# Moving the low parts of the key, query and rotated-head evacuations into the weight stream of a two-layer hybrid decoder kernel

## The chip, the cores and the metric

One core of a Trainium2 chip runs the whole kernel. The metric is the device time of one execution in microseconds (us); 1863.25 us is the median of three runs before the change (1862.83 to 1863.87).

## The reference, cut to what matters

Two layers over a sequence of 1024 tokens with 1024 channels. Each layer norms the stream, projects it by one wide matrix, feeds four mixers (stick-breaking attention, a grouped state-space model called S5, retention, and a gated linear recurrence called RG-LRU), gates and projects each mixer's output, sums them and projects once more.

```python
h = _rms_norm(x, pre_g)
proj = jnp.einsum('bsd,dc->bsc', h, w_in)
sb_qkv, ssm_u, ret_qkv, lru_u, gates, merge = jnp.split(proj, SPLITS, axis=-1)
...
# stick-breaking attention, per block of 128 queries
q = q.astype(jnp.float32) * (d ** -0.5)
z = jnp.einsum('bhqd,bhkd->bhqk', q[:, :, lo:hi], k[:, :, :hi])
...
# retention: q and k are rotated first
return jnp.concatenate([t1 * cos - t2 * sin, t1 * sin + t2 * cos], axis=-1)
```

## The kernel before, in words

The work is cut into four units, one for each layer and half sequence of 512 tokens: unit 0 (layer 0, first half), unit 1 (layer 0, second half), unit 2 and unit 3 (layer 1). A unit is a fixed series of 64 weight tiles, i = 0 to 63, of 1024 or 1280 columns each, handled by `filler` (L1133). Every product is made three times in a reduced-precision float (`mm3`, L1110): high part of the activations by high part of the weights, low by high, high by low. So each half tile of weights is loaded by SyncE, and then split by `split` (L106): ScalarE copies it to the high part `wh` (L86), VectorE subtracts that from the raw weights and writes the low part `wl` (L89). There are five buffers for each part. `ahead(g, hf)` (L207) keeps this stream three half tiles ahead of TensorE: at half tile s it issues the split of half tile s+3. In a half tile of 12 matmuls the third is the first that reads `wl`.

This text numbers half tiles within a unit: tile i has the halves 2i and 2i+1. So the split of half 27 (second half of tile 13) is issued at the start of tile 12, that of half 28 in the middle of tile 12.

All engines work in the order in which the code emits their instructions. Around a tile this is: the steps of the side generators that a hand-written plan (`PLAN`, L1475) puts at the start of the tile; the split of the first half and 12 matmuls; the split of the second half, `mid` (L1453, more side steps) and 12 matmuls; then the evacuation of the finished PSUM bank. The tiles that matter here are:

- i = 8 and 10 (L1165): keys of stick-breaking attention. ScalarE copies two high halves into `kS` (L1172), VectorE subtracts two low halves (L1176).
- i = 9 and 11 (L1179): queries. ScalarE makes eight scaled copies of 64 x 128 (L1195), VectorE makes eight scaled duplicates (`ts`, L1197) and eight low parts (`stt`, L1199). Eight more ScalarE copies of the low parts (`rest`, L1201) are kept in `S["late"]` and emitted in the `mid` of the next tile.
- i = 12 to 15 (L1225): queries and keys of retention, rotated. ScalarE makes four shifted copies (L1237), VectorE multiplies by the cosine (L1238), multiplies the shifted copy by the sine (L1239) and adds (L1240).

The stick-breaking attention `sba` (L989) is started at i = 12. At the start of tile 12 TensorE makes the scores of the first block and head, and ScalarE two sigmoids of each segment (L1040, L1041), with a table load in front. In the middle of tile 12 VectorE makes the scans and products on them (L1053 to L1059). At the start of tile 14 TensorE transposes the result (L1019). The second head follows from tile 14 on in the same way. The RG-LRU steps (`lru`, L706) and S5 steps (`s5`, L768) lie between them; in unit 0 also the preparation of the S5 tables (`prep`, L468) with transposes at L630.

The queries, keys and rotated heads use PSUM banks from `A` (three buffers), tile 8 one from `B` (five buffers).

Of the kernel before, what the change touches and what calls it, by code (L numbers as in the profile page):

```python
# [9 lines left out]
F32 = mybir.dt.float32  # L10
# [4 lines left out]
ALU = mybir.AluOpType  # L15
# [28 lines left out]
def hybrid_kernel(ctx: ExitStack, tc: tile.TileContext, x, xt, ws1, ws2, par, bcw, preg, postg, con, rot, out, dbg=None):  # L44
# [17 lines left out]
    def nm(s):  # L62
        cnt[0] += 1
        return f"{s}{cnt[0]}"

    def G(dt=F32, w=512):
        return genp.tile([P, w], dt, tag="g", name=nm("g"))

    def A():
        return psa.tile([P, 512], F32, tag="a", name=nm("pa"))  # L70
# [8 lines left out]
    def Bdone(n=1):  # L79
        bopen[0] -= n  # L80

    def actv(out, in_, func, **kw):
        act.activation(out, in_, func, **kw)  # L83

    def copy(out, in_, **kw):
        act.activation(out, in_, AF.Copy, **kw)  # L86

    def tt(out, a, b, op):
        dve.tensor_tensor(out, a, b, op=op)  # L89

    def ts(out, a, s1, s2=None, op0=ALU.mult, op1=None):
        if s2 is None:
            dve.tensor_scalar(out, a, s1, None, op0=op0)  # L93
        else:
            dve.tensor_scalar(out, a, s1, s2, op0=op0, op1=op1)

    def stt(out, a, s, b, op0, op1):
        dve.scalar_tensor_tensor(out, in0=a, scalar=s, in1=b, op0=op0, op1=op1)  # L98

    def mm(out, lhsT, rhs, start=True, stop=True):  # L100
        pe.matmul(out, lhsT=lhsT, rhs=rhs, start=start, stop=stop)  # L101
# [4 lines left out]
    def split(src, hi, lo):  # L106
        copy(hi, src)
        tt(lo, src, hi.bitcast(F32), ALU.subtract)
# [19 lines left out]
    kS = [const.tile([P, SEQ], F32R, name=f"kS{h}") for h in range(4)]  # L128
# [28 lines left out]
    def tile_of(u, i):  # L157

        if i < GATE0:
            return 0, i  # L160
        if i >= WOUT0:
            return 0, i - 4 * 8
        n, j = group(u, i), (i - GATE0) % GRP
        return (1, 8 * n + j - 2) if j >= 2 else (0, GATE0 + 2 * n + j)
# [6 lines left out]
    def load_to(g):  # L171
        while nload[0] <= min(g, ntot - 1):
            u, i = divmod(nload[0], NTILE)
            kind, idx = tile_of(u, i)
            src = (ws1, ws2)[kind]
            w = 2 * HALF[kind]
            t = rawp.tile([P, w], F32, tag="raw", name=nm("raw"))
            if nload[0]:
                sp.dma_start(t, src[units[u][0], idx])
            else:  # L180
                for hf in range(2):
                    sp.dma_start(t[:, hf * w // 2:(hf + 1) * w // 2], src[units[u][0], idx][:, hf * w // 2:(hf + 1) * w // 2])
            raws[nload[0]] = t
            nload[0] += 1

    def split_to(s):
        while nsplit[0] <= min(s, 2 * ntot - 1):
            g, hf = divmod(nsplit[0], 2)
            load_to(g)
            kind = tile_of(*divmod(g, NTILE))[0]  # L190
            w = HALF[kind]
            hi = whp.tile([P, w], F32R, tag="wh", name=nm("wh"))
            lo = wlp.tile([P, w], F32R, tag="wl", name=nm("wl"))
            split(raws[g][:, hf * w:(hf + 1) * w], hi[:, :], lo[:, :])
            his[nsplit[0]] = hi
            los[nsplit[0]] = lo
            if hf:
                raws.pop(g)
            nsplit[0] += 1
# [7 lines left out]
    def ahead(g, hf):  # L207
        load_to(g + 3)
        split_to(2 * g + hf + 3)

    def wdone(g):
        for s in (2 * g, 2 * g + 1):
            his.pop(s)
            los.pop(s)


    S = {}


    def prologue(u):  # L220
# [64 lines left out]
    def set_h(hh, hl):  # L285
        S["h"] = ([hh[:, k, :] for k in range(KD)], [hl[:, k, :] for k in range(KD)])

# [23 lines left out]
    def prologue_t(c):  # L311
        gc = S["par", 0][:, C_PG:C_PG + 8]
        xk = [G() for _ in range(KD)]
# [30 lines left out]
    def first():  # L344
        pr = S["par", 0] = parp.tile([P, NPAR], F32, tag="par", name=nm("par"))
        gc = pr[:, C_PG:C_PG + 8]
# [17 lines left out]
        for k in range(KD):  # L364
# [8 lines left out]
            if k < 4:  # L373
                sqs.append(G())
                actv(sqs[k], xk[k], AF.Square)
        S["h"] = (xh, xl)
        yield 0
# [17 lines left out]
        for k in range(0, KD, 2):  # L395
# [6 lines left out]
            if k == 2:  # L402
                set_h(hh, hl)
                for t in range(2):
                    dve.memset(uext[t][:, 0:3], 0.0)
                    tt(uext[t][:, 3:3 + T], S.pop(("lps", t)), rb, ALU.mult)
                    S["uext", t] = True
                    Bdone()
# [714 lines left out]
    def coltile(g, mid, side=False):  # L1123
        ps = B() if side else A()
        for hf in range(2):
            ahead(g, hf)
            if hf:
                mid()
            for k in range(4 * hf, 4 * hf + 4):
                mm3(ps, g, k * P, P, False, hsl(k), k == 0, k == 7)  # L1130
        return ps

    def filler(u, i, mid):  # L1133
        l, c = units[u]
        g = u * NTILE + i
# [14 lines left out]
        elif i < 4:  # L1150
            t = i - 2
            ps = coltile(g, mid, i == 2 or u == 0)
# [12 lines left out]
        elif i in (8, 10):  # L1165
            pq = i // 10
            ps = coltile(g, mid, i == 8)
            for h2 in range(2):
                k_ = kS[2 * pq + h2]
                a = slice(64 * h2, 64 * h2 + 64)  # L1170
                cs = slice(ts0, ts0 + T)
                copy(k_[a, cs], ps[a, :])  # L1172
            for h2 in range(2):
                k_ = kS[2 * pq + h2]
                a, b = slice(64 * h2, 64 * h2 + 64), slice(64 - 64 * h2, 128 - 64 * h2)
                tt(k_[b, cs], ps[a, :], k_[a, cs].bitcast(F32), ALU.subtract)  # L1176
            if i == 8:
                Bdone()
        elif i in (9, 11):  # L1179
            pq = i // 11  # L1180
            ps = coltile(g, mid)
            todo = []
            for b in range(NT):
# [4 lines left out]
                for h2 in range(2):  # L1188
                    a = slice(64 * h2, 64 * h2 + 64)
                    h = 2 * pq + h2  # L1190
                    hs_ = slice(h * P, (h + 1) * P)
                    o = slice(64 - 64 * h2, 128 - 64 * h2)
                    todo.append((qh[a, hs_], qh[o, hs_], ql[a, hs_], ql[o, hs_], ps[a, sl]))
            for q_, _, _, _, z in todo:
                copy(q_, z, scale=0.125)  # L1195
            for _, qd, _, _, z in todo:
                ts(qd, z, 0.125)  # L1197
            for q_, _, r_, _, z in todo:
                stt(r_, z, 0.125, q_.bitcast(F32), ALU.mult, ALU.subtract)  # L1199

            def rest():  # L1201
                for _, _, r_, rd, _ in todo:
                    copy(rd, r_.bitcast(F32))

            S["late"] = rest
        elif i < 8:
            if i == 4:
                S["vps"] = [A(), A(), A(), B()]
# [7 lines left out]
            if i == 7:  # L1216
                ps = S.pop("vps")
# [7 lines left out]
        elif i < GATE0:  # L1225
            j = i - 12
            pq, isk = divmod(j, 2)
# [4 lines left out]
            ps = coltile(g, mid)  # L1232
            cs, sn = S["rot"]
            sw, r = G(), G()
            for b in range(4):
                a = b ^ 1
                copy(sw[32 * b:32 * b + 32, :], ps[32 * a:32 * a + 32, :])  # L1237
            tt(r, ps, cs, ALU.mult)  # L1238
            tt(sw, sw, sn, ALU.mult)  # L1239
            tt(r, r, sw, ALU.add)  # L1240
            S[("rk" if isk else "rq"), pq] = r
            if j == 3:
                S.pop("rot")
# [1 line left out]
        elif i < WOUT0:  # L1245
            n, j = group(u, i), (i - GATE0) % GRP
            if j < 2:
                ps = coltile(g, mid)
# [8 lines left out]
            else:  # L1257
                d = j - 2
# [22 lines left out]
        else:  # L1281
# [32 lines left out]
            else:  # L1314
                ps = S["ops"]
                o, st = S["o"]
# [81 lines left out]
    todo = {}  # L1398
# [27 lines left out]
    with tc.manual_schedule():  # L1426
        dve.memset(ones1, 1.0)
        warm = G(BF16)
        dve.memset(warm, 0.0)
        ps = A()  # L1430
        for _ in range(NWARM):
            mm(ps, warm[:, 0:P], warm)
        start("first", first())
        for t in (tmat, ore, oim, wll):
            pool.memset(t if t is not wll else t.bitcast(F32), 0.0)
        for u, (l, c) in enumerate(units):
            for i in range(NTILE):
                if u == 0 and i == 8:
                    copy(identb, ident)
                    copy(trib, cons[:, K_TRI:K_TRI + P])  # L1440
                if i == 12:
                    start("sb", sba(l, c))
                if i == 28 and c == 1 and l + 1 < DEPTH:
                    load_par(l + 1)
                for name, f in (("post", WOUT0), ("prep", NTILE if u else 24), ("lru", GATE0), ("s5", GATE0 + (1 if u else 2) * GRP),
                                ("ret", GATE0 + (2 if u else 1) * GRP), ("sb", GATE0 + 3 * GRP)):
                    if i == f:
                        drain(name)

                sb_now = i % 2 == 0  # L1450
                hfree[0] = i > WOUT0

                def mid():  # L1453
                    finish_gate()
                    if "late" in S:
                        S.pop("late")()
                    step("first")
                    if sb_now:
                        step("sb")
                    planned(u, 2 * i + 1)  # L1460

                if sb_now:
                    step("sb")
                planned(u, 2 * i)
                filler(u, i, mid)
                step("first")
            drain("prep")
            drain("pro")
# [157 lines left out]
```

## Time and profile before

| | |
|---|---|
| median of three runs | 1863.25 us |
| the profiled execution's own time | 1862.88 us |
| its span, first to last instruction | 1861.1 us |
| TensorE (PE) busy | 1826.2 us, 98% |
| VectorE (DVE) busy | 1200.8 us, 65% |
| ScalarE (ACT) busy | 888.2 us, 48% |
| GpSimd (POOL) busy | 258.1 us, 14% |
| mean granted TensorE clock | 0.995 |

A busy share is an average over stages: an engine that is busy 65% of the span can be the bound for 30 us on end. A row of a timeline gives the start, the duration, the engine, the line, what is written from what, and in brackets how long the engine had stood idle before and which engine's instruction ended that. A row that ends in x8 stands for eight instructions in a row.

### The profile page before, as it was taken

What the parts mean: (1) busy time and instruction counts of PE and PEld (TensorE: products, weight loads), DVE (VectorE), ACT (ScalarE), POOL (GpSimd) and SP (SyncE); (2) the same over time, 40 slices, a digit from 0 to 9 for tenths busy, and PEclk for the clock granted to TensorE, in tenths of its full rate; (3) what the DMA queues carried; (4) which work ended last, traced back from release to release, by engine and by line L of the source; (5) the groups of instructions that cost most, each with busy time, mean ns of one, the idle gap of its engine ahead of it and who ended that gap; (6) DMA issues with size and microseconds to landing.
All of it is one profiled execution on the core that took longest, in us unless ns stands there. A gap on an engine that the chain in (4) does not pass through costs nothing.

```text
span 1861.1 us, 24840 instructions
## 1 busy us (share of the span) xinstructions
PE 1826.2 (98%) x9210; PEld 1508.6 (81%) x9210; DVE 1200.8 (65%) x2168; ACT 888.2 (48%) x1673; POOL 258.1 (14%) x573
## 2 busy tenths in 40 slices
PE   9989999999999999999999999999999999999997
PEld 6767888888888888888888788888888788888886
DVE  7777755455689576744558856656437895676445
ACT  5773444344476444544546543344353845444333
POOL 6891000020000002893000000000000000000001
PEclk9999999999999999999999999999999999999999
DMA  5231232324333222232434322242243323222232
GB/s 177 99 119 48 71 125 87 125 94 154 104 132 103 89 81 71 87 135 91 145 112 136 100 90 95 78 138 99 94 139 123 118 85 102 69 78 71 99 105 102
DMA packets 68856, 193.95 MB, mean 104 GB/s; under 512 B 9600, under 2 KB 18176, under 8 KB 68736
## 3 DMA queue, kind: packets, MB, share of 16 engines
q1 hardware_dynamic: 68736, 192.38, 30.9%
q8 instruction: 72, 1.18, 0.3%
q14 instruction: 48, 0.39, 0.1%
HBM read 179.11 MB, written 12.58 MB: 103 GB/s over the span
## 4 chain that ended last, share of the span: by engine, by line
PE 85%; DVE 8%; ACT 5%; issue 1%; DMA 1%; SPq 0%; DVEq 0%; ACTq 0%
PE pa L101 66%; PE pb L101 16%; DVE g L89 2%; PE pb L1019 2%; ACT g L86 2%; ACT g L83 1%; DVE wl L89 1%; DVE g L98 1%; DVE g L93 1%; ACT wh L86 1%; DMA raw<-in_ws_dram 1%; DVE g L810 0%; PE pb L254 0%; ACT kS L86 0%; DVE g L1057 0%
## 5 line engine op out<-in xcount | busy, mean ns | idle before, releaser
L101 PE MATMUL pa<-hh,wl 128*128 128x512 f32 x1576 | 616.2, 391 | 13.3 <-DVE wl L89 13.3
L101 PE MATMUL pa<-hh,wh 128*128 128x512 f32 x1576 | 624.1, 396 | 0.1
L101 PE MATMUL pa<-hl,wh 128*128 128x512 f32 x1576 | 615.0, 390 | 0.0
L89 DVE TENSOR_TENSOR wl<-raw,wh 128x512 fp32r<-128x512 f32 (+1 forms) x512 | 374.7, 770 | 196.0 <-ACT wh L86 195.2
L89 DVE TENSOR_TENSOR g<-g,g 128x512 f32<-128x512 f32 (+7 forms) x435 | 298.8, 687 | 124.3 <-ACT g L86 104.6
L86 ACT ACTIVATE wh<-raw 128x512 fp32r<-128x512 f32 (+1 forms) x512 | 328.3, 686 | 85.6 <-PE pb L101 42.5
L101 PEld LDWEIGHTS pa<-hh,wl 128*128 128x128 f32 x1576 | 296.6, 188 | 80.0 <-DVE wl L89 16.7
L101 PEld LDWEIGHTS pa<-hh,wh 128*128 128x128 f32 x1576 | 296.7, 188 | 61.3 <-ACT wh L86 0.5
L101 PEld LDWEIGHTS pa<-hl,wh 128*128 128x128 f32 x1576 | 296.9, 188 | 58.3 <-DVE hl L89 0.2
L83 ACT ACTIVATE g<-pa 128x512 f32<-128x512 f32 x161 | 96.3, 598 | 507.1 <-PE pa L101 464.6
L89 DVE TENSOR_TENSOR g<-g,pa 128x512 f32<-128x512 f32 x128 | 87.6, 685 | 189.6 <-PE pa L101 171.2
L101 PE MATMUL pa<-g,wh 128*128 128x512 f32 x544 | 169.2, 391 | 2.4 <-ACT g L83 1.1
L905 POOL MEMSET g<- 128x512 f32 x8 | 4.0, 526 | 938.2 <-PE pb L101 937.1
L86 ACT ACTIVATE g<-pb 128x512 f32<-128x512 f32 (+4 forms) x163 | 72.8, 472 | 123.6 <-PE pb L101 88.4
L101 PEld LDWEIGHTS pa<-g,wh 128*128 128x128 f32 x544 | 102.0, 188 | 26.6 <-ACT g L83 1.9
L86 ACT ACTIVATE g<-g 128x512 fp32r<-128x512 f32 (+2 forms) x152 | 79.3, 522 | 72.6 <-DVE g L89 34.9
L101 PE MATMUL pa<-g,wl 128*128 128x512 f32 x272 | 106.0, 390 | 0.0
L83 ACT ACTIVATE g<-pb 128x512 f32<-128x512 f32 (+4 forms) x203 | 87.9, 513 | 22.4 <-PE pb L101 19.6
L86 ACT ACTIVATE g<-pa 64x128 fp32r<-64x128 f32 (+3 forms) x150 | 69.1, 461 | 34.5 <-PE pa L101 32.9
L101 PE MATMUL pa<-wh,g 128*128 128x512 f32 x256 | 79.5, 392 | 0.0
L101 PE MATMUL pb<-wh,g 128*128 128x512 f32 x256 | 79.1, 391 | 0.0
L83 ACT ACTIVATE g<-g 128x512 f32<-128x512 f32 (+2 forms) x98 | 57.1, 602 | 31.1 <-DVE g L89 22.8
(215 smaller groups left out, 2093.8 us busy)
## 6 DMA issues: line engine op xcount, KB each, us to landing
raw<-in_ws_dram SPq DMA_DIRECT2D x128, 640.0 KB, 3.9
raw<-in_ws_dram SPq DMA_DIRECT2D x127, 512.0 KB, 3.7
g<-x SPq DMA_DIRECT2D x32, 256.0 KB, 5.9
g<-in_xt_dram SPq DMA_DIRECT2D x16, 256.0 KB, 6.7
g<-in_x_dram SPq DMA_DIRECT2D x16, 256.0 KB, 3.1
x<-g SPq DMA_DIRECT2D x16, 256.0 KB, 2.1
out_dram<-g SPq DMA_DIRECT2D x16, 256.0 KB, 2.0
g<-in_rot_dram SPq DMA_DIRECT2D x8, 256.0 KB, 4.3
```

What stands on the lines that cost most here:

```text
L83: act.activation(out, in_, func, **kw)
L86: act.activation(out, in_, AF.Copy, **kw)
L89: dve.tensor_tensor(out, a, b, op=op)
L93: dve.tensor_scalar(out, a, s1, None, op0=op0)
L98: dve.scalar_tensor_tensor(out, in0=a, scalar=s, in1=b, op0=op0, op1=op1)
L101: pe.matmul(out, lhsT=lhsT, rhs=rhs, start=start, stop=stop)
L905: pool.memset(t, 0.0)
L1019: pe.transpose(ps[:, q * P:(q + 1) * P], r[:, q * P:(q + 1) * P], ident)
```

## The change

The low parts are no longer emitted at once after the high copies. They are put into a list, and `ahead` takes one entry from it at each half tile, right after the split of that half tile. A query tile gives three entries: low parts and duplicates of the first two blocks; those of the last two blocks and the four ScalarE copies for the first two; the four ScalarE copies for the last two. A key tile gives one entry (both subtractions), a rotated tile one (sine product and sum). The copies no longer wait for `mid`. No instruction is added or removed.

```diff
     def ahead(g, hf):
         load_to(g + 3)
         split_to(2 * g + hf + 3)
+        if S["later"]:
+            S["later"].pop(0)()
...
-            for h2 in range(2):
-                k_ = kS[2 * pq + h2]
-                a, b = slice(64 * h2, 64 * h2 + 64), slice(64 - 64 * h2, 128 - 64 * h2)
-                tt(k_[b, cs], ps[a, :], k_[a, cs].bitcast(F32), ALU.subtract)
-            if i == 8:
-                Bdone()
+
+            def lows():
+                for h2 in range(2):
+                    k_ = kS[2 * pq + h2]
+                    a, b = slice(64 * h2, 64 * h2 + 64), slice(64 - 64 * h2, 128 - 64 * h2)
+                    tt(k_[b, cs], ps[a, :], k_[a, cs].bitcast(F32), ALU.subtract)
+                if i == 8:
+                    Bdone()
+
+            S["later"].append(lows)
...
             for q_, _, _, _, z in todo:
                 copy(q_, z, scale=0.125)
-            for _, qd, _, _, z in todo:
-                ts(qd, z, 0.125)
-            for q_, _, r_, _, z in todo:
-                stt(r_, z, 0.125, q_.bitcast(F32), ALU.mult, ALU.subtract)
-
-            def rest():
-                for _, _, r_, rd, _ in todo:
-                    copy(rd, r_.bitcast(F32))
-
-            S["late"] = rest
+
+            def share(o, d):
+
+                def run():
+                    for q_, _, r_, _, z in o:
+                        stt(r_, z, 0.125, q_.bitcast(F32), ALU.mult, ALU.subtract)
+                    for _, qd, _, _, z in o:
+                        ts(qd, z, 0.125)
+                    for _, _, r_, rd, _ in d:
+                        copy(rd, r_.bitcast(F32))
+                return run
+
+            S["later"] += [share(todo[:4], []), share(todo[4:], todo[:4]), share([], todo[4:])]
...
             tt(r, ps, cs, ALU.mult)
-            tt(sw, sw, sn, ALU.mult)
-            tt(r, r, sw, ALU.add)
+
+            def turn():
+                tt(sw, sw, sn, ALU.mult)
+                tt(r, r, sw, ALU.add)
+
+            S["later"].append(turn)
...
                 def mid():
                     finish_gate()
-                    if "late" in S:
-                        S.pop("late")()
                     step("first")
```

## Rows read from the trace of the kernel before

**Rows 1.** The page: busy time of each engine, share of the span, instructions.
```profile
PE 1826.2 (98%) x9210; PEld 1508.6 (81%) x9210; DVE 1200.8 (65%) x2168; ACT 888.2 (48%) x1673; POOL 258.1 (14%) x573
```

**Rows 2.** Whom TensorE waited for: us in total, times, longest us.
```profile
PE pa L101 <- DVE wl L89: 13.5, 8, 4.2
```

**Rows 3.** Timeline of TensorE in unit 1, tiles 13 and 14.
```profile
555.99 0.50 PE L101 MATMUL pa<-hh,wl 128*128 128x512 f32 x1 [0.87 <-DVE wl L89]
...
558.16 0.39 PE L101 MATMUL pa<-hh,wl 128*128 128x512 f32 x1
559.44 0.76 PE L1019 MATMUL pb<-cons,g 128*128 128x128 f32 x5 [0.89 <-DVE g L89]
```

**Rows 4.** Timeline of ScalarE in unit 1, tiles 9 to 12.
```profile
538.07 2.57 ACT L86 ACTIVATE g<-g 64x128 fp32r<-64x128 f32 x8 [1.60 <-DVE g L98]
...
547.97 2.26 ACT L86 ACTIVATE g<-pa 64x128 fp32r<-64x128 f32 x8
550.25 1.28 ACT L83 ACT_TABLE_LOAD   x1
551.54 1.43 ACT L83 ACTIVATE g<-pb 128x512 f32<-128x512 f32 x4
552.83 1.17 ACT L86 ACTIVATE wh<-raw 128x512 fp32r<-128x512 f32 x2
```

**Rows 5.** Timeline of VectorE in unit 1, from tile 11's evacuation on.
```profile
550.26 2.40 DVE L93 TENSOR_SCALAR g<-pa 64x128 fp32r<-64x128 f32 x8 [1.81 <-ACT g L86]
552.68 2.53 DVE L98 SCALAR_TENSOR_TENSOR g<-pa,g 64x128 fp32r<-64x128 f32 x8
555.25 1.29 DVE L89 TENSOR_TENSOR wl<-raw,wh 128x512 fp32r<-128x512 f32 x2
556.46 0.42 DVE L1057 TENSOR_TENSOR_SCAN g<-g,ones 128x127 f32<-128x127 f32 x1
...
558.69 0.69 DVE L89 TENSOR_TENSOR g<-g,g 128x511 f32<-128x511 f32 x1
```

**Rows 6.** Timeline of TensorE in unit 3, start of tile 14.
```profile
1473.98 0.76 PE L1019 MATMUL pb<-cons,g 128*128 128x128 f32 x5 [0.88 <-DVE g L89]
```

**Rows 7.** Timeline of TensorE in unit 2, tiles 12, 13 and start of 14.
```profile
1021.46 0.39 PE L101 MATMUL pa<-hl,wh 128*128 128x512 f32 x1
...
1024.18 0.39 PE L101 MATMUL pa<-hl,wh 128*128 128x512 f32 x1
1028.80 0.80 PE L101 MATMUL pa<-hh,wl 128*128 128x512 f32 x1 [4.23 <-DVE wl L89]
...
1032.54 0.27 PE L1019 MATMUL pb<-cons,g 128*128 128x128 f32 x1
```

**Rows 8.** Busy us by stretch: PE, PEld, DVE, ACT, POOL; then granted PE clock, DMA.
```profile
1028.00:1028.50 0.50, 0.00 (x0) 0.00 (x0) 0.50 (x2) 0.48 (x2) 0.00 (x0) 0.78 0.00 0
```

**Rows 9.** Timeline of VectorE in unit 2, tile 12.
```profile
1025.29 0.69 DVE L98 SCALAR_TENSOR_TENSOR g<-g,g 128x512 f32<-128x512 f32 x1
...
1028.07 1.28 DVE L89 TENSOR_TENSOR wl<-raw,wh 128x512 fp32r<-128x512 f32 x2
...
1029.72 0.29 DVE L89 TENSOR_TENSOR g<-g,g 128x127 f32<-128x127 f32 x1
```

**Rows 10.** Timeline of TensorE in unit 0, tiles 13 to 17.
```profile
97.78 0.66 PE L630 MATMUL pb<-cons,ore 128*128 128x128 f32 x4 [1.40 <-ACT ore L86]
117.91 0.50 PE L101 MATMUL pa<-hh,wl 128*128 128x512 f32 x1 [2.91 <-DVE wl L89]
126.04 0.50 PE L101 MATMUL pa<-hh,wl 128*128 128x512 f32 x1 [2.39 <-DVE wl L89]
```

**Rows 11.** Timeline of VectorE in unit 0, tiles 13 to 15.
```profile
102.10 1.41 DVE L89 TENSOR_TENSOR g<-g,g 128x512 f32<-128x512 f32 x2
108.05 1.30 DVE L89 TENSOR_TENSOR wl<-raw,wh 128x512 fp32r<-128x512 f32 x2 [4.54 <-ACT wh L86]
114.05 2.36 DVE L89 TENSOR_TENSOR g<-g,g 128x512 f32<-128x512 f32 x2
```

More of the change, by code (lines that the diff above doesn't have):

```diff
@@ L214, in wdone @@
             los.pop(s)
-    S = {}
+    S = {"later": []}
     def prologue(u):
```

## The prediction

> **What bounds the kernel now.** I read the page first, then the list of what TensorE waited for, then the timelines of the three engines around each wait. The page says that TensorE is busy for 98% of the span [rows 1], so of 1861 us only about 35 are idle, and no change on another engine can win more than a part of these. The list of waits says who holds most of what can be named: VectorE's low weights `wl`, 13.5 us in eight waits [rows 2]. The timelines show where: all behind the evacuations that the change touches. One is in unit 2 (4.23 [rows 7]) and one each in units 1 and 3 (0.87 [rows 3]; unit 3 repeats unit 1's pattern). The other 7.5 us are in unit 0, 2.91 and 2.39 of them at tiles 16 and 17 [rows 10].
>
> In unit 1 the query tile 11 leaves eight duplicates and eight low parts on VectorE, 2.40 and 2.53 us, and only then comes `wl` of half 27, at 555.25 [rows 5]. TensorE stood 0.87 us for it [rows 3]. In unit 2 it is the same queue with an RG-LRU step of 2.8 us (1025.29 to 1028.07) in it too [rows 9]. There the wait also cost clock: the granted clock fell to its half (1.2 of 2.4 GHz) shortly after 1028, which the 0.78 of that half microsecond shows [rows 8], and the ten matmuls from 1028.80 to 1032.54 took 3.74 us; at their usual 0.227 (twelve from 1021.46 to 1024.18 in 2.72) they take 2.27. The wait of 4.39 start to start and this 1.47 make 5.9 us [rows 7].
>
> But a second wait stands close behind, in units 1 and 3: at the start of tile 14 TensorE needs the scans of the stick-breaking attention, which follow on VectorE behind the same evacuation. It stood 0.89 us for them at 559.44 [rows 3] and 0.88 in unit 3 [rows 6]. That wait decides this change.
>
> **The change, part by part.** No instruction and no DMA is added or taken away, so no engine's busy time moves; SyncE's loads are issued in the same order, and the raw buffers of the second halves come free at most a share (2.47 us, below) later, which I cost at nothing: a tile of 24 matmuls (5.4 us) lies between a load and its use. If that cover went, the price would be up to 2.5 us once a unit.
>
> *The query shares, units 1 and 3.* A share is four low parts and four duplicates: a half of 2.40 + 2.53 us, so 2.47 [rows 5]. Before, VectorE's order after tile 11's copies was: 4.93 of evacuation, 1.29 for the two `wl`, 2.95 of scans (556.46 to 559.38) [rows 5]. After, it is `wl` 27, share, `wl` 28, share, scans: the same 9.1 us in another order. `wl` 27 is then no longer late. The start of this stretch, however, moves. The old one starts as soon as ScalarE has ended the eight query copies (550.23, and VectorE had stood 1.81 us for that [rows 4, 5]). The new one starts with `wl` 27, which needs `wh` 27; and on ScalarE this stands behind the table load (1.28) and four sigmoids (1.43) of the first scores: it ends near 553.4, 3.2 us after the query copies [rows 4]. A share cannot overtake the `wl` ahead of it. VectorE, which used to work in the shadow of the sigmoids, stands there.
>
> Against this, ScalarE itself runs earlier. It stood 1.60 us before tile 9's second copies, waiting for low parts [rows 4]; now the first `stt` comes ahead of the duplicates, and the copies are asked for a share later. I reckon 1.0 of the 1.60 won, with ends of 0 and 1.6. So the stretch starts 3.2 - 1.0 = 2.2 us later, and so do the end of the scans (559.4 to 561.6) and TensorE's transposes at tile 14. Everything up to there that TensorE gains by `wl` 27 being ready, it only waits for longer: it arrives near 557.5 (558.16 + 0.23 - 0.87) and stands 4.1 us. **Loss in unit 1: 2.2 us (1.6 to 3.2); in unit 3 the same.** Behind the waiting share stand also `wl` 28 and the PSUM bank of tile 11, which tile 14 takes over; both are free some 3 us before the scans end, so they are covered by the longer wait.
>
> *The query shares, unit 2.* VectorE's rows there show no idle time up to the end of the scan at 1030.0 [rows 9]: it is late by itself, `wh` lies ready, and the new order starts no later. `wl` 27 comes in front of the 4.93 us, at 1028.7 - 4.9 = 1023.8; TensorE wants it at 1024.4 [rows 7]. The 5.9 us go. Next late is again the scan: the same work stands ahead of it as before, so it ends at 1030.0. TensorE, arriving at 1026.7 (ten matmuls after 1024.4), stands 3.3 us for it, and starts tile 14 at 1030.05 instead of 1032.54. **Gain in unit 2: 2.5 us** (2.0 to 2.9).
>
> *Unit 0.* The two early waits for `wl` go, but TensorE then arrives earlier at the transposes of 97.78, where it already stood 1.40 us for ScalarE's copies of the S5 tables [rows 10]; these come perhaps 0.6 us earlier, from ScalarE's idle time before the second copies. For the two late waits the *rotated-head part* counts. From 108.05 VectorE is full up to `wl` 33 and 35. The sum of tile 13 (1.41) used to be done at 102.10, in time that VectorE otherwise spent waiting for `wh` 31 (4.54 idle); now it stands behind that wait, in the full stretch. The sum of tile 14 (2.36 there) goes behind `wl` 33, that of tile 15 behind `wl` 35 [rows 11]. For `wl` 33 this is 2.36 - 1.41 = 0.95 better, for `wl` 35 about 0.4. With the 0.6: **gain in unit 0: 1.0 us** (0 to 2).
>
> *The key part.* Two subtractions of 0.69 us later by a half tile; their readers come two tiles later. Nothing, in units 1 to 3 hidden by VectorE's waits for ScalarE; without that cover 1.4 us a key tile on VectorE alone.
>
> *The clock.* The new waits of 4.1 us (units 1, 3) lie next to the one of 4.23 in which the clock fell [rows 7, 8]; that one fall, late in its wait, is all that the trace has, and after the wait of 2.91 us there was none: its first matmul shows 0.50 us, that of 1028.80 shows 0.80 [rows 7, 10]. I take half the price of 1.47 for each, 1.4 in all; ends 0 and 4.4 (all three new waits).
>
> Sum: -1.0 + 2.2 - 2.5 + 2.2 + 1.4 = **+2.3 us**. The profiled execution took 1862.88 (1861.1 of span, 1.8 around it), so 1865.2; the median of the runs is 0.37 above it: **1865.6 us**.
>
> On the table load the Trainium skill speaks more strongly against the change. The row shows the load taking 1.28 us and the first sigmoid starting right after it, at 551.54 [rows 4]. The page "ScalarE: Activation LUTs", section "What ACT_TABLE_LOAD costs", adds a drain of about 1.38 us to each switch. If that held, the new stretch would start another 1.4 us later in units 1 and 3, and the sum would be about +5; the trace disagrees, and I go by the row.
>
> **The rivals.**
>
> *No new wait (12%).* If the scans were ready when TensorE reaches tile 14, all named waits there would go: 0.87 + 0.89 in unit 1, the like in unit 3, 5.9 in unit 2, and 2 in unit 0: about -11, 1852 us. For it: the `wl` waits are the biggest group [rows 2]. Against: 4.9 us of shares must still pass VectorE ahead of the scans, and TensorE was already waiting for these.
>
> *Half (20%).* ScalarE gets ahead by the whole 3.2 us in units 1 and 3 (the sigmoids no longer hold `wh` 27), so nothing is lost there, and units 0 and 2 gain 3.5: 1859.8 us. For it: ScalarE's waits for VectorE before tile 11. Against: more than the 1.60 us seen [rows 4] would have to be won.
>
> *Slower, by the clock (25%).* The waits in units 1 to 3 are all followed by half clock: +4.4 in place of 1.4, so +5.3, 1868.5 us. It decides where ScalarE wins less than the 1.0 us that I give it, so that TensorE's new waits grow past the 4.23 of unit 2, and in unit 2 where the scan ends later than now. The Trainium skill's "TensorE: Matmul & The Clock Gate", Part 1, has the clock halved by an idle engine; the trace agrees, once, in unit 2 [rows 7, 8].
>
> *The change does not do what it says (3%).* An entry is taken only once per half tile, so key and rotated parts queue behind three query shares; were a reader to come first, TensorE would wait for it at tile 12. The first reads are of blocks in the first share, two tiles later. Within 1 us of now.
>
> **How the numbers follow.** My forecast has 40%. The range must take in the ends of the parts (all good: -2 - 2.9 + 3.2 = -1.7; all bad: 0 - 2 + 6.4 + 4.4 = +8.8, which I don't expect together) and reach to the half case: **1859.5 to 1869.5**. Left out are the first rival and the far bad end. A measurement of this kernel tells about 0.2%, 3.7 us, from no change: below 1859.5 is faster, above 1867.0 slower. Faster: the first rival and a little of the second, 0.15. Slower: the clock rival and the upper end of my own, 0.30. Within: 0.55.
>
> **What would show it.** In the profile of the changed kernel: no wait for `wl` in units 1 to 3; TensorE at the transposes of tile 14 (L1019) waiting some 4 us for VectorE in units 1 and 3 and 3 in unit 2; VectorE idle for about 3.5 us in unit 1 ahead of `wl` 27, ended by ScalarE's `wh`; low parts of tile 11 starting after 552 instead of ending at 555. In unit 0 waits for `wl` at tiles 16 and 17 that are still there. I am wrong if the list shows neither `wl` nor L1019 among the long waits, or if ScalarE reaches `wh` 27 by 550.3.

## The result and the profile after

The changed kernel took 1870.78 us, the median of 6 runs (1869.41 to 1875.65), beside 1862.88 us for the kernel before (6 runs, 1859.91 to 1863.87): a ratio of 1.0052, interval 1.0041 to 1.0063. It is slower by 7.9 us in the medians (9.7 in the means, which is what the ratio compares), where 2.3 were predicted.

The profiled execution took 1869.92 us, span 1868.0. The page's busy times are those of before [rows 1] to within 2.5 us:

```profile
PE 1827.3 (98%) x9210; PEld 1510.8 (81%) x9210; DVE 1203.3 (64%) x2168; ACT 887.9 (48%) x1673; POOL 257.6 (14%) x573
```

So no engine has more to do; the order costs the time. The list of what TensorE waited for answers to [rows 2] (us in total, times, longest). The lines of the code moved by two: L1021 is what was L1019, the transposes of the attention's weights, and L1059 are the scans.

```profile
PE pb L1021 <- DVE g L89: 18.0, 6, 4.7
PE pa L101 <- DVE wl L89: 3.8, 3, 2.6
PE pb L101 <- DVE g L89: 2.9, 3, 1.8
...
PE pa L101 <- DVE kS L89: 0.9, 1, 0.9
```

In the kernel before the transposes stood in this list with

```profile
PE pb L1019 <- DVE g L89: 1.8, 2, 0.9
```

The 13.5 us for `wl` have become 3.8, and the transposes' 1.8 have become 18.0. TensorE's timeline shows where, in units 0, 1, 2 and 3 in turn:

```profile
87.56 0.47 PE L101 MATMUL pa<-hh,wh 128*128 128x512 f32 x1 [0.87 <-DVE kS L89]
96.05 0.33 PE L1021 MATMUL pb<-cons,g 128*128 128x128 f32 x1 [2.77 <-DVE g L89]
...
113.52 0.30 PE L1021 MATMUL pb<-cons,g 128*128 128x128 f32 x1 [1.75 <-DVE g L89]
120.04 0.50 PE L101 MATMUL pa<-hh,wl 128*128 128x512 f32 x1 [2.63 <-DVE wl L89]
127.21 0.50 PE L101 MATMUL pa<-hh,wl 128*128 128x512 f32 x1 [1.04 <-DVE wl L89]
...
555.73 0.39 PE L101 MATMUL pa<-hh,wl 128*128 128x512 f32 x1
560.77 1.33 PE L1021 MATMUL pb<-cons,g 128*128 128x128 f32 x5 [4.65 <-DVE g L89]
...
565.09 0.63 PE L101 MATMUL pa<-hl,wh 128*128 128x512 f32 x1
...
565.87 0.40 PE L101 MATMUL pa<-hh,wh 128*128 128x512 f32 x1
...
1033.47 0.47 PE L1021 MATMUL pb<-cons,g 128*128 128x128 f32 x1 [3.47 <-DVE g L89]
...
1479.13 1.12 PE L1021 MATMUL pb<-cons,g 128*128 128x128 f32 x4 [4.65 <-DVE g L89]
```

In unit 1 nothing is waited for at tile 13 any more [rows 3], and the time saved is waited for at tile 14, with 3.8 us more. VectorE says why [rows 5]:

```profile
551.48 0.69 DVE L89 TENSOR_TENSOR wl<-raw,wh 128x512 fp32r<-128x512 f32 x1 [3.68 <-ACT wh L86]
552.09 1.24 DVE L98 SCALAR_TENSOR_TENSOR g<-pa,g 64x128 fp32r<-64x128 f32 x4
553.36 1.20 DVE L93 TENSOR_SCALAR g<-pa 64x128 fp32r<-64x128 f32 x4
554.57 0.69 DVE L89 TENSOR_TENSOR wl<-raw,wh 128x512 fp32r<-128x512 f32 x1
...
560.02 0.69 DVE L89 TENSOR_TENSOR g<-g,g 128x511 f32<-128x511 f32 x1
```

It stands 3.68 us for `wh` 27 while the shares lie ready behind that wait. ScalarE has the table load and the sigmoids in front of `wh` 27, and only 0.77 us of lead over before (1.27 us of the 2.04 between 548.21 here and 550.25 [rows 4] is this execution's lead up to there):

```profile
548.21 1.28 ACT L83 ACT_TABLE_LOAD   x1
549.50 1.43 ACT L83 ACTIVATE g<-pb 128x512 f32<-128x512 f32 x4
550.79 1.18 ACT L86 ACTIVATE wh<-raw 128x512 fp32r<-128x512 f32 x2
```

And the granted clock falls in that wait and stays down after it (windows of 5 us: the stretch and its length; the busy time of TensorE, of its weight loads, of VectorE, ScalarE and GpSimd; then the clock, and two columns of DMA):

```profile
555.00:560.00 5.00, 1.11 (x5) 0.57 (x4) 4.71 (x14) 4.79 (x11) 0.00 (x0) 0.90 0.01 3
560.00:565.00 5.00, 4.23 (x14) 3.75 (x15) 4.88 (x8) 3.90 (x10) 0.00 (x0) 0.50 0.36 121
565.00:570.00 5.00, 5.00 (x22) 4.05 (x21) 4.89 (x9) 0.44 (x1) 0.00 (x0) 0.92 0.21 46
```

0.50 is 1.2 of 2.4 GHz. TensorE restarts at 560.77, and its matmuls last 0.63 instead of 0.39 us until 565.87.

### The profile page after: what moved, and what is told of

Its sections match the earlier page's. It is cut to its first block, busy times and chain, and to the rows that moved or that the text cites. A ratio compares the mean times of both kernels' runs of the same rounds, so it can differ in the third digit from the quotient of the medians.

```text
span 1868.0 us, 24849 instructions
## 1 busy us (share of the span) xinstructions
PE 1827.3 (98%) x9210; PEld 1510.8 (81%) x9210; DVE 1203.3 (64%) x2168; ACT 887.9 (48%) x1673; POOL 257.6 (14%) x573
## 4 chain that ended last, share of the span: by engine, by line
PE 85%; DVE 7%; ACT 4%; issue 1%; DMA 1%; SPq 0%; DVEq 0%; ACTq 0%
PE pa L101 67%; PE pb L101 15%; DVE g L89 2%; PE pb L1021 2%; DVE g L98 2%; DVE wl L89 1%; ACT g L86 1%; ACT g L83 1%; DMA raw<-in_ws_dram 1%; ACT wh L86 1%; DVE g L93 1%; ACT L83 0%; PE pb L256 0%; DMA ubuf<-g 0%; DVE g L1059 0%
```

## The experiments

Theory A is the prediction's mechanism: a share can't overtake the split ahead of it, so VectorE idles in the sigmoids' shadow and tile 12's scans come late; TensorE pays once for the wait and once more in clock. Rival B: dividing the evacuations costs by itself, or the loss lies in the key and rotated-head parts. The kernel before took 1863.38 us (median of 24 executions) beside the first four experiments, and 1862.23 us beside the others.

Where several kernels are compared, a table helps: the time from the start of tile 14's transposes to the start of tile 16's (the rows of L1019, or L1021 and L1024 where lines have moved; the clock shows here), in brackets TensorE's wait just before.

| kernel | unit 1 | unit 2 | unit 3 |
|---|---|---|---|
| before | 12.31 (0.89) | 11.36 (none) | 12.31 (0.88) |
| changed | 14.65 (4.65) | 12.98 (3.47) | 14.60 (4.65) |
| TensorE kept busy | 12.36 (0.69) | 11.46 (0.96) | 12.32 (0.69) |
| split 27 first | 13.88 (2.33) | 12.73 (3.99) | 13.94 (2.33) |
| share ahead of split | 12.32 (1.95) | 11.49 (1.30) | 13.91 (1.95) |

**The query shares alone.** Key low parts and rotated sums at once, as before:

```
-            S["later"].append(lows)
+            lows()
...
-            S["later"].append(turn)
+            turn()
```

> Only the query shares are put off; keys and rotated heads are evacuated at once, as before. Theory A (the query shares stand behind the low weights of half 27, the scans come 2.6 us later in units 1 and 3, and TensorE's clock halves in the longer wait): the whole loss is there, 1870 to 1872 us, waits for the scans at the start of tile 14 of 4 to 5 us in units 1 and 3. Theory B (the loss comes from the keys and rotated heads that hold PSUM banks and lengthen VectorE's stretches): back near 1863 us.

Measured: 1873.37 us (1870.41 to 1876.6), ratio 1.0058, interval 1.0045 to 1.007. The waits at the transposes are 4.67, 3.79 and 4.67 us. The whole loss is in the query shares. By the medians it is 2.1 us more than the change's and 1.4 us over the expected range, though the two intervals overlap. Of the 6.7 us between the two traces 3.2 are a fall of the clock in unit 0 that the last section tells of, and 2.6 lie in unit 2: there VectorE is full (no idle time in [rows 9]), the sums and subtractions that are not put off stand ahead of the scans, and the transposes come 1.4 us later (after taking off each kernel's offset at the unit's start, 8.24 and 3.15 us):

```profile
1039.94 0.48 PE L1021 MATMUL pb<-cons,g 128*128 128x128 f32 x1 [3.79 <-DVE g L89]
```

That unit lost 2.0 us to the kernel before, where the changed kernel's won 0.6.

**Keys and rotated heads alone.** The reverse: the query tiles are evacuated as before.

```
-            S["later"] += [share(todo[:4], []), share(todo[4:], todo[:4]), share([], todo[4:])]
+            for _, qd, _, _, z in todo:
+                ts(qd, z, 0.125)
...
+            S["late"] = rest
```

> The other half alone: only key subtractions and rotated sums are put off, the query evacuations stay as before. Theory A: 1861.5 to 1864.5 us, waits for the low weights in units 1 to 3 as before (0.9, 4.2, 0.9). Theory B: most of the loss, 1868 us or more.

Measured: 1865.98 us (1863.68 to 1868.37), ratio 1.0016, interval 1.0007 to 1.0025: a small loss of its own, 1.5 us over the expected range. In each of units 1 to 3 TensorE loses some 0.7 us behind the second query tile:

```profile
558.25 0.50 PE L101 MATMUL pa<-hh,wl 128*128 128x512 f32 x1 [1.60 <-DVE wl L89]
```

That wait was 0.87 [rows 3]. The put-off key subtraction (1.39 us for two) now stands on VectorE ahead of the first query tile's work, and ScalarE's copies and the table load follow 0.7 us later. My "nothing" for the key part was wrong by this; the cover that I named, VectorE's waits for ScalarE, doesn't hide it, since ScalarE waits for VectorE in turn (1.60 us in [rows 4]).

**Split 27 ahead of the sigmoids.** To the changed kernel:

```
+                if i == 12:
+                    split_to(2 * (u * NTILE + i) + 3)
                 if sb_now:
                     step("sb")
```

> The changed kernel with one split moved: that of half 27 is issued ahead of the stick-breaking scores and their sigmoids at the start of tile 12 of every unit. Theory A: in units 1 and 3 VectorE no longer stands 3.7 us ahead of this subtraction, the scans end 2.5 us earlier, TensorE's wait there falls from 4.65 to about 2.2 us, and the clock stays full, which gives 2.3 more: about 4.9 us a unit, 1861 us (1859 to 1863.5). Theory C (ScalarE's order is of no account, VectorE is simply full): 1869 us or more.

Measured: 1866.64 us (1863.22 to 1868.31), ratio 1.0018, interval 1.0009 to 1.0026. The order on VectorE and TensorE's wait came out as theory A has them, and the loss went from 7.9 to 3.3 us. VectorE in unit 1 stands only 1.10 us for `wh` 27:

```profile
548.07 0.69 DVE L89 TENSOR_TENSOR wl<-raw,wh 128x512 fp32r<-128x512 f32 x1 [1.10 <-ACT wh L86]
```

and TensorE half as long as in the changed kernel:

```profile
557.61 0.74 PE L1021 MATMUL pb<-cons,g 128*128 128x128 f32 x5 [2.33 <-DVE g L89]
```

The expected range (1859 to 1863.5) was missed by 3.1 us: the clock, expected to stay full, fell after these waits too (1.6 us in the table for units 1 and 3), and unit 2's wait of 3.99 us remained. In this execution units 1 to 3 lose 2.3 us to the kernel before. It is the quickest of the eleven, at 1863.22 us and a mean granted clock of 0.995; the median one has 0.991, so a part of its loss lies in falls of the clock that this trace does not show.

**TensorE kept busy.** To the changed kernel, matmuls whose result is overwritten, so many that they fill most of the new wait:

```
+                    if i == 1 and o == 0:
+                        for _ in range((0, 17, 12, 17)[l * NCH + c]):
+                            mm(ps, identb, S["h"][0][0])
```

> The changed kernel with 17, 12 and 17 matmuls more (128 x 512, results overwritten) ahead of the transposes at tile 14 of units 1, 2 and 3, 3.9, 2.7 and 3.9 us in waits of 4.65, 3.47 and 4.65. The waits themselves stay. If the half clock after these waits is a cost of its own, 2.3 + 1.6 + 2.3 us are won: 1864 to 1865.5 us, with full clock in these stretches. If it only fills time that VectorE takes anyway, 1870 to 1871 us.

Measured: 1868.33 us (1864.53 to 1869.99), ratio 1.0026, interval 1.0015 to 1.0036. Nothing that the program needs is earlier, and yet it is faster than the changed kernel. The windows of unit 1 show what is left out, the half clock:

```profile
558.00:563.00 5.00, 5.00 (x24) 4.01 (x22) 4.72 (x14) 4.79 (x11) 0.00 (x0) 1.00 0.07 25
563.00:568.00 5.00, 4.31 (x23) 3.40 (x22) 4.87 (x9) 3.98 (x10) 0.00 (x0) 1.00 0.29 100
568.00:573.00 5.00, 5.00 (x23) 4.13 (x22) 4.90 (x8) 2.46 (x6) 0.00 (x0) 1.00 0.22 50
```

In the table the three stretches are those of before to within 0.1 us each, against 2.34, 1.62 and 2.29 us more in the changed kernel. So the clock is a price of its own, 6.2 us in these stretches. Some 0.9 us of it came back later in units 1 and 3, and unit 2's transposes begin 0.7 us later here than in the changed kernel, so between the two traces units 1 to 3 are 4.7 us shorter. The medians give 3.0 us for it (7.9 less 4.95), the ratios 4.8 (1.0052 less 1.0026, of 1863). I had expected the whole 6.2 and 1864 to 1865.5 us, 2.8 too little. In unit 0, which this edit leaves as it was, this execution took 3.1 us more than that of the changed kernel, at the fall that the last section tells of.

**Each share ahead of its split.** To the changed kernel:

```
         load_to(g + 3)
-        split_to(2 * g + hf + 3)
         if S["later"]:
             S["later"].pop(0)()
+        split_to(2 * g + hf + 3)
```

> The changed kernel with the share of each half tile put ahead of that half tile's weight split instead of behind it. Theory A (the loss comes from the scans of tile 12, which stand behind two shares and two splits on VectorE): VectorE works share 1 in the 3.68 us in which it waited for the sigmoids and split 27's high half, so the scans of units 1 and 3 end some 2.5 us earlier, TensorE's wait ahead of the transposes of tile 14 falls from 4.65 to about 2.2 us there, and in unit 2 from 3.47 to about 1.5 us, with split 27 about 2 us late at tile 13. With waits of that length the half clock afterwards costs less than in the changed kernel. Time 1861 to 1866 us. Rival B (the loss is in the many small pieces themselves, wherever they stand): 1869 us or more.

Measured: 1861.07 us (1859.39 to 1863.12), ratio 0.9995, interval 0.9986 to 1.0004. The loss is gone with one line moved; all the small pieces are still there, so rival B falls as the cause of it. VectorE in unit 1 now works its first share in the sigmoids' shadow and stands 0.78 us for `wh` 27 instead of 3.68:

```profile
552.57 0.69 DVE L89 TENSOR_TENSOR wl<-raw,wh 128x512 fp32r<-128x512 f32 x1 [0.78 <-ACT wh L86]
```

TensorE's waits are 1.95 us in units 1 and 3 and 1.30 in unit 2. The two equal waits differ in what follows, unit 1's first, then unit 3's:

```profile
559.38 0.77 PE L1021 MATMUL pb<-cons,g 128*128 128x128 f32 x5 [1.95 <-DVE g L89]
...
1472.08 1.09 PE L1021 MATMUL pb<-cons,g 128*128 128x128 f32 x5 [1.95 <-DVE g L89]
```

The windows behind them:

```profile
560.00:565.00 5.00, 5.00 (x26) 4.20 (x25) 4.89 (x8) 4.94 (x12) 0.00 (x0) 1.00 0.38 131
...
1472.00:1477.00 5.00, 4.92 (x19) 4.23 (x20) 4.86 (x9) 4.91 (x12) 0.00 (x0) 0.66 0.40 133
```

In unit 1 the clock held, in unit 3 it fell, for 1.6 us.

**The scans ahead of the late share.** From here the kernel before is the base. In the second query tile, split 27 stands first (by the two lines of the third experiment), half of the heads are evacuated behind it, and the other half behind the scans:

```
+                S["later"].append(share(h0, [], h0))
+                S["tail"] = share(h1, todo, h1)
...
                     if sb_now:
                         step("sb")
+                    if i == 12:
+                        S.pop("tail")()
```

> The kernel before, with three edits for the second query tile alone: split 27 ahead of the stream's step at tile 12, the first four heads' share behind split 27 (in the stretch in which VectorE waits for the sigmoids), and the other four behind the scans in the middle of tile 12. Keys, rotated heads and the first query tile as before. Theory A: in units 1 and 3 the scans end some 2.5 us earlier than with split 27 first alone (there 557.46), about 555.0, so TensorE, which comes to tile 14 at about 555.3, doesn't wait for them; what is left is some 0.5 us for the PSUM bank that the late share holds. In unit 2 the waits come to about 3 us in place of 4.23 us. Sum against the kernel before: -1.3 -1.1 -1.3 and a unit 0 that is open: 1857 to 1861 us. Rival B (any division of the query work costs): no faster than the kernel before, 1863 us or more.

Measured: 1868.32 us (1866.2 to 1870.56), ratio 1.0031, interval 1.0019 to 1.0043, where 1857 to 1861 were expected: wrong. By the number alone it would fit rival B (1863 or more). Tile 14 did begin earlier (1.6 us in unit 1), with a wait of 0.43 us at its transposes, but the next transposes came 16.21 us later instead of 12.31, at a granted clock of 1.00 throughout. ScalarE shows the new wait:

```profile
559.33 0.95 ACT L86 ACTIVATE g<-g 64x128 fp32r<-64x128 f32 x3 [2.61 <-DVE g L98]
...
560.61 2.39 ACT L86 ACTIVATE g<-pa 32x512 f32<-32x512 f32 x4
```

The copies of the late share's low parts wait for VectorE, and the rotated-head copies of tile 12, whose matmuls had ended near 553.3, stand behind them. The Trainium skill, "PSUM — Partial Sum Buffer", section "Engine vs sequencer instructions", says that ScalarE's and VectorE's queues are strictly first in, first out; the row shows what that costs.

**The same, with four copies on ScalarE.**

```
+                def dup():
+                    for _, qd, _, _, z in h1:
+                        copy(qd, z, scale=0.125)
...
+                S["later"] += [share(h0, [], h0), dup]
+                S["tail"] = share(h1, todo, [])
```

> As the run before, with the four copies of the query's high half of the late share taken from VectorE to ScalarE, behind the high half of split 28. The PSUM bank is then free 1.2 us earlier: in units 1 and 3 no wait at tile 14, in unit 2 about 1.8 us. Theory A: 1 to 2 us under the run before, 1855 to 1860 us. Rival: ScalarE's extra 1.1 us ahead of its rotated-head copies is late for the stream, and nothing is won over the run before.

Measured: 1869.22 us (1867.98 to 1871.75), ratio 1.0037, interval 1.0025 to 1.005. Nothing is won over 1868.32, as the rival had it: ScalarE, whose queue is the blocked one, got more to do. The next run tests that it is.

**The low copies out of ScalarE's way.** To the kernel with the scans ahead of the late share:

```
-                S["later"].append(share(h0, [], h0))
-                S["tail"] = share(h1, todo, h1)
+                S["later"] += [share(h0, [], h0), share([], h0, [])]
+                S["tail"] = share(h1, [], h1)
+                S["rest"] = share([], h1, [])
...
+                    if i == 14:
+                        S.pop("rest")()
```

> As the run with the scans ahead of the second share, but the ScalarE copies of that share's low halves are queued in the middle of tile 14 and not behind the share itself. Theory: there the loss came from ScalarE, which waited 2.61 us for the late share's first subtraction with the rotated-head copies of tile 12 queued behind that wait, so that these began at 560.61; with the low copies out of the way they begin at about 556.7, the following tiles' evacuations aren't late, and the 3.9 us that units 1 and 3 lost between tiles 14 and 16 go, as do some of those in units 0 and 2: 1857 to 1861 us. Rival: the delay came from VectorE, which took up the late share's 2.5 us ahead of the rotated heads' products, and 1865 us or more remain.

Measured: 1862.4 us (1860.33 to 1865.11), ratio 1.0001, interval 0.9992 to 1.001. The 5.9 us between this and 1868.32 are what ScalarE's blocked queue cost. The rotated-head copies of tile 12 start 6.3 us earlier (2.4 of it is the offset between the two executions at the unit's start):

```profile
554.31 2.39 ACT L86 ACTIVATE g<-pa 32x512 f32<-32x512 f32 x4
```

It doesn't beat the kernel before all the same, and its expectation was missed by 1.4 us: tile 14 starts 1.6 us earlier in units 1 and 3, and that and some 0.7 us more is given back by tile 16, to a PSUM bank that the late share holds and to the next scans:

```profile
559.15 0.47 PE L101 MATMUL pa<-hh,wh 128*128 128x512 f32 x1 [0.93 <-DVE g L93]
571.25 0.74 PE L1021 MATMUL pb<-cons,g 128*128 128x128 f32 x5 [0.95 <-DVE g L89]
```

**Split 27 first, and nothing else.** The kernel before with the two lines of the third experiment.

> The kernel before with nothing changed but split 27 ahead of the stream's step at tile 12. It tells what that order is worth by itself. The wait of 0.87 us in units 1 and 3 for split 27's low half goes, and in unit 2 the one of 4.23 us becomes about 1.4 us, but the scans are no earlier, so that TensorE waits for them at tile 14 by about what it had won in unit 2: 1860 to 1863.5 us. If it is the whole of what the run with the late share wins, the late share wins nothing.

Measured: 1860.42 us (1859.18 to 1863.26), ratio 0.9988, interval 0.9979 to 0.9996. It has the lowest median of all, 1.8 us under the kernel before, though not in the way expected. The wait in unit 1 is still there, 0.83 us: split 27's low half still stands behind the query tile's 4.93 us on VectorE. In the trace units 1 to 3 are level with before; what is won is in unit 0. The wait of 2.39 us at tile 17 [rows 10] is shorter there:

```profile
126.54 0.50 PE L101 MATMUL pa<-hh,wl 128*128 128x512 f32 x1 [1.03 <-DVE wl L89]
```

But nothing is won by that: the matmul starts at 126.54 instead of 126.04, and this execution was behind by the same 0.5 us before the two late waits. TensorE only came to the wait later, since its clock had fallen at 118 us. What is won comes after it, where the execution of before ran partly at half clock (0.66 from 126 to 131 us, 0.81 from 165 to 170) and this one did not:

```profile
126.00:131.00 5.00, 4.46 (x23) 3.42 (x24) 4.93 (x8) 1.30 (x4) 4.92 (x8) 1.00 0.85 260
165.00:170.00 5.00, 3.60 (x28) 3.47 (x29) 1.78 (x4) 1.07 (x2) 0.00 (x0) 1.00 0.00 0
```

The second stretch and the 10 us behind it make 1.7 us. The other executions agree: their mean granted clocks are 0.995 to 0.997, those of the kernel before 0.993 to 0.995. So the win goes with the clock; by what the edit would keep it up, no run here shows.

## Why the prediction was wrong

**The mechanism held.** `wl` is waited for in none of units 1 to 3; the transposes of tile 14 wait 4.65, 3.47 and 4.65 us, where some 4.1, 3.3 and 4.1 were predicted; VectorE idles 3.68 us ahead of `wl` 27, where 3.5 were predicted, ended by `wh`; the low parts of tile 11 start at 552.09, after the 552 that was named. The first, second and fifth experiment show each link: the query shares carry the loss, they carry it by the scans, and moving the share ahead of the split takes it away.

**The step that failed is the clock**, a term of the sum that was mis-sized twice over. I took half of 1.47 us for each of the new waits in units 1 and 3, 1.4 in all, and nothing for the new wait in unit 2. It fell in all three, and each fall cost more: the stretches of the table are longer by 2.34 + 1.62 + 2.29 = 6.2 us. The 1.47 was counted over ten matmuls after a wait of 4.23, of which the last three were already at full clock, from 3.0 us past the restart on; after the new waits the half clock lasted 5.1, 3.4 and 5.0 us past the restart. The far end of my bounds, 4.4, was itself too low, because it multiplied that one price by three. The fourth experiment shows the term by itself.

The reading under the half was wrong, too. The fall in unit 2 is not all that the trace of before has: another stands right behind the wait of 2.39 us at 126.04 [rows 10], and one behind a wait of 1.85 us at 166.56 (last section). The clock of the first is 0.66:

```profile
126.00:131.00 5.00, 4.96 (x19) 3.42 (x20) 4.93 (x8) 1.63 (x4) 4.92 (x8) 0.66 0.86 280
```

**Scans, units 1 and 3:** +2.6 us each against 2.2. In the frame of before (1.27 us later) the scans end at 561.98 instead of 559.38. ScalarE won 0.77 of its wait and not the 1.0 that I gave it; the rest is small. **Unit 2:** -2.2 for the scan against -2.5; TensorE starts tile 14 at 1033.47, which in the frame of before (3.15 us earlier) is 1030.3, against 1030.05. Both are sound.

**Unit 0:** +1.6 us up to 150 us instead of -1.0, a wrong sign. The two early waits for `wl` went, as I said, but in their place came waits of 2.77 and 1.75 for the scans and of 0.87 for a PSUM bank that the put-off key subtraction (kS) holds. I had costed the key part at nothing and hadn't looked at unit 0's scans. The second experiment alone loses 1.0 us there. Each of the executions of before and after also has a fall of the clock in this stretch, at 127 and at 98 us, and what these two cost is not taken out.

**The Trainium skill's drain** ("ScalarE: Activation LUTs", section "What ACT_TABLE_LOAD costs") again isn't in the row: the sigmoids begin 1.29 us after the table load does. Going by the row was right, though the +5 that the rule gave lay closer to the result, for another reason.

**The sum**, in the profiled execution: -1.2 (start-up, different in each execution), +1.6 (unit 0), -1.7 (a fall of the clock in unit 0 that the execution of before had and this one didn't), +5.2 - 2.2 (scans), +6.2 (clock), -0.9 (won back later in units 1 and 3) make +7.0, and 1869.92 less 1862.88 is 7.04. Of the rivals, the one by the clock came nearest, 0.25 of the chance, and its condition was met (ScalarE won 0.77 and not 1.0, the waits grew to 4.65); its price was too small as well, and the clock fell after unit 2's shorter wait, too. The range ended 1.3 us short of the result.

## What to carry to other kernels

In an in-order queue, putting work behind "the next thing that is urgent" also puts it behind whatever that thing waits for; before moving it, see whether the queue now works in the shadow of that wait. Moving the share one line up took the whole loss away, and letting ScalarE's copies wait for a late share cost 5.9 us in the same manner. A new wait of TensorE has to be priced with the clock behind it: where it fell in the stretches of the table, that cost 1.4 to 2.3 us on top of waits of 2.0 to 4.7.

## What the runs showed of the hardware that was not expected

- The length of the wait alone doesn't tell whether the clock falls. At the waits of the table it held after 0.7 to 1.3 us, fell each time after 2.33 and more, and after 1.95 it held once and fell once in one execution (fifth experiment). In unit 0 it held after longer ones: after 2.91 us at 117.91 in the kernel before [rows 10], and after 2.63 us at 120.04 in the changed kernel. Their windows, in this order:

```profile
117.00:122.00 5.00, 4.09 (x18) 3.40 (x19) 4.97 (x6) 4.14 (x9) 4.75 (x6) 1.00 0.11 32
119.00:124.00 5.00, 3.86 (x16) 2.88 (x17) 4.97 (x7) 1.40 (x4) 4.92 (x8) 1.00 0.01 3
```

  The Trainium skill, "TensorE: Matmul & The Clock Gate", Part 1, warns, for a kernel's first matmuls, that the same kernel meets the gate differently from run to run; these runs agree, and not for the first matmuls alone (the executions of the kernel before have mean granted clocks of 0.993 to 0.995, and the fall in the next point comes in some only).
- It also falls without a long wait, in unit 0 after a wait of 1.8 us ahead of 24 small matmuls, in seven of the eleven profiled executions and not in the others, with code that no kernel here changes. The first row is the kernel before, where the granted clock was 0.81 from 165 to 170 us:

```profile
166.56 4.00 PE L101 MATMUL pb<-g,g 128*128 128x128 f32 x24 [1.85 <-DVE g L89]
```

The second is the changed kernel, with 1.00:

```profile
166.95 2.89 PE L101 MATMUL pb<-g,g 128*128 128x128 f32 x24 [1.83 <-DVE g L89]
```

  Between these two executions it made 1.65 us, so one profiled execution against another can be off by this much in a place that the change doesn't touch; medians of several runs and a comparison stretch by stretch are both needed.
- Waits of two engines for one another pass a delay on. Two subtractions of 0.69 us a half tile later (second experiment) cost 0.7 us in each of three units, though both VectorE and ScalarE had idle time beside them.
